# Issuing the delta-rule branch's output inside the state-space scan, with a tile tag of its own for the merge gate

## The chip, the cores and the metric

The kernel runs on one core of a Trainium2 chip, as one launch. The metric is the device time of that launch in microseconds, the median of several runs. Smaller is better.

## The reference, cut to what matters

One layer: a half-step SwiGLU feed-forward, a token mixer, a second half-step feed-forward, with 256 latent and 256 context tokens of 1024 channels. The change touches the end of the mixer only: two branches (a gated delta rule, result `o`, and a Mamba-2 state-space scan, result `y`) are gated, normalised, projected, and merged by sigmoid gates.

```python
def mixer_out(f, o, y, gdn_norm_g, mb_d, mb_norm_g, w_branch_gdn, w_branch_mb, w_out):
    za = f['zA'].reshape(b, n, GDN_HEADS, GDN_DV)
    ya = (rmsnorm(o, gdn_norm_g) * jax.nn.silu(za)).astype(dt).reshape(b, n, GDN_V)
    yb = y + mb_d.reshape(MB_GROUPS, MB_HPG)[..., None] * f['xs']
    yb = yb.reshape(...) * jax.nn.silu(f['zB'].reshape(...))
    yb = rmsnorm(yb, mb_norm_g.reshape(...)).astype(dt).reshape(b, n, MB_INNER)
    ga, gb = jnp.split(f['gates'], 2, axis=-1)
    merged = jax.nn.sigmoid(ga) * (ya @ w_branch_gdn) + jax.nn.sigmoid(gb) * (yb @ w_branch_mb)
    return merged @ w_out
```

`zA`, `zB` and `gates` are slices of the input projection `h @ w_in`.

## The kernel before, in words

**How the order comes about.** The mixer is written as a set of steps, and the string `PLAN` lists them. A number ahead of a slash sets the priority of all that follows; a smaller number goes first. The steps are issued in the order of `PLAN`, and a list scheduler then fills each engine's queue from what is ready, smaller numbers first. Two things follow from the order of issue and not from the numbers: tiles of one tag take their slots as the steps ask for them, and a step whose tile has no free slot waits for the holder. Each engine afterwards works through its own queue strictly in order, and so does SP, which starts most DMAs.

**The steps at the end of the mixer.**
- `zB5`, `g17`, `zA9` run the projections of the gates at priority 30. Each of the eight units of `zA` is eight matmuls into a PSUM tile of tag `mm` (two banks), then `zth` on ACT and DVE (L1067, L1068), then a write of `zAsc` to DRAM.
- `h40` runs the generator `ssd_all` to its end. It works on four quarters (`gi`, `hf`): `ssd_off` (state `pSs`, the sum `yg` with `xlat`, the terms `pyo` and `yo`), two `ssd_diag` (tiles `Es`, filled by a DMA from `asd`, worked on by POOL at L1429, DVE at L1431, ACT, DVE at L1442 and L1444, then the matmuls `pyd`), and `ssd_gate` (`zt`, L1456). After the second and the fourth quarter `ssd_norm` scales two quarters (`yr0`, `yr1`, L1468). The generator yields 40 times.
- `y0`, `y1` are `ssd_out`: four rounds each. A round is four transposes on PE into `pyb` (PSUM tag `tr`, one bank), then twice `ybH` on ACT (L1506) and `ybL` on DVE (L1507).
- `gdn_out` reads `zA` back from DRAM, makes `ya`, its rounded half `yaH` (ACT, L1295) and the rest `yaL` (POOL, L1296), runs the eight projections `wbg` (24 matmuls each, into `acc` of tag `mm`), and merges each with its gate `ga` into `mg` (L1302).
- `mb_out` runs the sixteen units of `wbm` against `ybH` and `ybL`, two to an accumulator, and adds `mg` (L1525, L1526).

`yg`, `xlat`, `yaH`, `yaL`, `ybH`, `ybL` and `mg` all take slots of one tag, `s4`, which has 16. `ga`, `gb`, `zA`, `zt` share tag `tL`, which has 2.

In the order lists below, a number behind a tile's name tells which tile of that name it is. `yg_8109` and `xlat_8110` are the fourth quarter's tiles before, `yg_8431` and `xlat_8432` after.

Of the kernel before, what the change touches and what calls it, by code (L numbers as in the profile page):

```python
# [6 lines left out]
F32 = mybir.dt.float32  # L7
# [7 lines left out]
P = 128  # L15
D = 1024
KD = 8
NL = 256
# [11 lines left out]
NCV = 2  # L30
POOLC = lambda t, s: False
PLAN = """10/k3 block_decay k6 5/elim 18/g5 13/dts 20/v2 g10 v7 13/m0 14/m1 13/chain_start s0 s1 m2 m3 22/q9
    B_part 27/x17 25/lat_h 22/C_part 30/zB5 g17 zA9 chain_out 13/s2 s3 14/gdn_norm 15/ssd_pre h40 51/y0 gdn_out y1 70/mb_out"""
NG = 5
GQ = 0
SSE = "gvg"
# [103 lines left out]
class Kernel:  # L140
# [1138 lines left out]
    def gdn_out(self):  # L1279

        nc, V = self.nc, self.nc.vector
        o, bc = self.o, self.bc
        yH = Ks(self, 8, NL, "yaH")
        yL = Ks(self, 8, NL, "yaL")
        for h2 in range(4):
            pv = self.smp([P, 2, NL], "pya", "ch")
            for j in range(2):
                for t in range(2):
                    nc.tensor.transpose(pv[:, j, t * P:t * P + P], o[t][:, 2 * h2 + j], self.ident)
            ya = self.t2([P, 2, NL], "ya")  # L1290
            j, hs = h2 // 2, slice(2 * (h2 % 2), 2 * (h2 % 2) + 2)
            zA = self.t2([P, 2, NL], "zA", tag="tL")
            nc.sync.dma_start(zA, self.zAsc[2 * h2:2 * h2 + 2].rearrange("m p n -> p m n"))
            V.scalar_tensor_tensor(out=ya, in0=pv, scalar=self.gng, in1=zA, op0=ALU.mult, op1=ALU.mult)
            nc.scalar.copy(yH.t[j][:, hs], ya)  # L1295
            (V if YAL[h2] == "v" else nc.gpsimd).tensor_tensor(yL.t[j][:, hs], ya, yH.t[j].bitcast(F32)[:, hs], op=ALU.subtract)  # L1296
        mg = self.mg = Ks(self, 8, NL, "mg", F32)
        for m in range(8):
            acc = self.proj("wbg", m, yH, yL, NL)
            ga = self.t2([P, NL], "ga", tag="tL")  # L1300
            nc.sync.dma_start(ga, self.gsc[m])
            V.scalar_tensor_tensor(out=mg[m], in0=ga, scalar=1.0, in1=acc, op0=ALU.add, op1=ALU.mult)  # L1302

# [329 lines left out]
```

## Time and profile before

| what | value |
| --- | --- |
| median of 3 runs | 1347.86 us (1344.52 to 1350.04) |
| the profiled execution | 1350.37 us, of it a span of 1348.6 us |
| mean granted TensorE clock in it | 0.973 |
| PE busy | 1267.5 us, 94% of the span |
| DVE busy | 977.1 us, 72% |
| ACT, POOL busy | 508.9 us (38%), 172.4 us (13%) |
| first unit of the last gate projections (`g`, then `zA`) | from 1003.87 us |
| first `wbg` matmul after the last read of `zA` | 1052.05 us |
| first merge with both `wbm` accumulators finished (L1525) | 1087.93 us |

Times inside the span count from its start. Rows of a timeline read: start, length, engine, line, operation, output, inputs, count, and in brackets the idle time just before and who ended it. The work around the change lies between about 860 and 1090 us.

### The profile page before, as it was taken

The numbers are of one execution on the slowest core, as the hardware profiler recorded it, in microseconds if no ns is written. First come the engines' busy times: TensorE is split into PE (matmuls) and PEld (weight loads), VectorE is DVE, ScalarE is ACT, GpSimd is POOL, SyncE is SP. The second block draws the span as 40 slices with busy tenths as digits, with TensorE's granted clock in tenths as the row PEclk, the third lists the DMA queues.
The fourth block names the chain that finished last, engine by engine and source line by source line (L and its number), as shares of the span: only waits on it lengthen the run. The fifth ranks groups of instructions, "written<-read, shape, count | busy, mean of one in ns | idle before, by whom it ended". The sixth has DMA issues, their size and how long they took to land.

```text
span 1348.6 us, 21052 instructions
## 1 busy us (share of the span) xinstructions
PE 1267.5 (94%) x8064; PEld 1083.8 (80%) x8064; DVE 977.1 (72%) x1692; ACT 508.9 (38%) x948; POOL 172.4 (13%) x130
## 2 busy tenths in 40 slices
PE   5889999999999997989998999998899899999997
PEld 3668888888899885779887888844468899999997
DVE  7998587646667966888778687997873466866565
ACT  3432122212236652345323565522223345544333
POOL 4200000000010231000122111333421001000000
PEclk9999999999999998999998999998999899999999
DMA  9256367636633398755542254554446556655552
GB/s 360 94 173 217 126 199 249 223 117 229 209 110 104 103 237 178 215 165 165 171 120 89 95 177 141 155 184 131 162 148 214 182 181 192 199 185 180 184 182 84
DMA packets 133016, 230.24 MB, mean 171 GB/s; under 512 B 46706, under 2 KB 78898, under 8 KB 132788
## 3 DMA queue, kind: packets, MB, share of 16 engines
q1 hardware_dynamic: 106240, 211.43, 49.7%
q10 hardware_dynamic: 26676, 17.47, 4.2%
q8 instruction: 63, 1.03, 0.3%
q14 instruction: 37, 0.30, 0.1%
HBM read 207.79 MB, written 21.07 MB: 170 GB/s over the span
## 4 chain that ended last, share of the span: by engine, by line
PE 63%; issue 17%; DVE 11%; DMA 7%; ACT 1%; POOL 1%; SPq 0%; ACTq 0%; DVEq 0%; POOLq 0%
PE acc L215 16%; PE acc L216 15%; PE acc L217 15%; PE acc L616 4%; PE acc L1054 2%; DVE junk L277 1%; DVE Es L1431 1%; DVE wlo L204 1%; PE pn L1232 1%; DMA zAsc<-zth 1%; DVE hL L440 1%; DMA Es<-asd 1%; DVE Es L1442 1%; PE pS L1258 1%; DMA raw<-in_wv 1%
## 5 line engine op out<-in xcount | busy, mean ns | idle before, releaser
L200 ACT CAST whi<-raw 128x1024 fp32r<-128x1024 f32 (+1 forms) x208 | 214.4, 1033 | 434.1 <-PE acc L216 369.4
L215 PE MATMUL acc<-hH,whi 128*128 128x512 f32 (+1 forms) x976 | 343.4, 358 | 17.2 <-ACT whi L200 8.3
L216 PE MATMUL acc<-hL,whi 128*128 128x512 f32 (+1 forms) x976 | 344.7, 355 | 4.6 <-DVE hL L440 4.6
L217 PE MATMUL acc<-hH,wlo 128*128 128x512 f32 (+1 forms) x976 | 343.3, 354 | 0.0
L204 DVE TENSOR_TENSOR wlo<-raw,whi 128x1024 fp32r<-128x1024 f32 (+1 forms) x208 | 254.4, 1225 | 93.3 <-ACT whi L200 92.0
L215 PEld LDWEIGHTS acc<-hH,whi 128*128 128x128 f32 x976 | 187.4, 192 | 43.0 <-ACT whi L200 8.6
L216 PEld LDWEIGHTS acc<-hL,whi 128*128 128x128 f32 x976 | 187.0, 192 | 30.5 <-DVE hL L440 6.9
L217 PEld LDWEIGHTS acc<-hH,wlo 128*128 128x128 f32 x976 | 186.3, 191 | 23.7
L277 DVE CUSTOM_DVE_ANT_0 junk<-wadat,cs 128x1024 f32<-128x1024 f32 x80 | 97.7, 1221 | 41.6 <-DMA wadat<-in_wadaT 40.9
L216 PE MATMUL acc<-aL,whi 128*128 128x256 f32 (+1 forms) x384 | 122.9, 323 | 0.0
L217 PE MATMUL acc<-aH,wlo 128*128 128x256 f32 (+1 forms) x384 | 122.3, 323 | 0.0
L215 PE MATMUL acc<-aH,whi 128*128 128x256 f32 (+1 forms) x384 | 122.3, 323 | 0.0
L616 PE MATMUL acc<-hF,raw 128*128 128x256 f32 x416 | 97.7, 391 | 14.6 <-ACT gth L1076 14.6
L635 DVE SCALAR_TENSOR_TENSOR cv<-cbuf,cc,cv 128x512 f32<-128x512 f32 (+1 forms) x144 | 102.0, 719 | 4.3 <-ACT cv L633 2.4
L616 PEld LDWEIGHTS acc<-hF,raw 128*128 128x128 f32 x416 | 80.3, 196 | 28.3 <-ACT gth L1076 16.0
L216 PEld LDWEIGHTS acc<-aL,whi 128*128 128x128 f32 x384 | 73.0, 190 | 5.7
L215 PEld LDWEIGHTS acc<-aH,whi 128*128 128x128 f32 x384 | 72.6, 190 | 5.7 <-DVE xc L572 0.2
L217 PEld LDWEIGHTS acc<-aH,wlo 128*128 128x128 f32 x384 | 72.7, 190 | 5.6
L382 POOL TENSOR_TENSOR sqa<-sqa,sqb 128x256 f32<-128x256 f32 x12 | 11.8, 981 | 430.5 <-ACT sqb L380 427.6
L572 DVE SCALAR_TENSOR_TENSOR xl<-acc,hg,xl 128x256 f32<-128x256 f32 x64 | 30.3, 481 | 47.3 <-PE acc L217 46.8
L1054 PE MATMUL acc<-raw,hF 128*128 128x512 f32 x128 | 59.4, 606 | 0.0
L1054 PEld LDWEIGHTS acc<-raw,hF 128*128 128x128 f32 x128 | 25.0, 197 | 30.2 <-issue 29.3
(398 smaller groups left out, 2082.3 us busy)
## 6 DMA issues: line engine op xcount, KB each, us to landing
raw<-in_wgu SPq DMA_DIRECT2D x76, 512.0 KB, 4.1
wadat<-in_wadaT SPq DMA_DIRECT2D x56, 512.0 KB, 4.1
raw<-in_wdn SPq DMA_DIRECT2D x44, 512.0 KB, 3.6
wada<-in_wada SPq DMA_DIRECT2D x16, 512.0 KB, 9.0
raw<-in_wg SPq DMA_DIRECT2D x16, 512.0 KB, 4.3
raw<-in_wxs SPq DMA_DIRECT2D x16, 512.0 KB, 3.4
Es<-asd SPq DMA_DIRECT2D x16, 512.0 KB, 4.3
raw<-in_wzB SPq DMA_DIRECT2D x16, 512.0 KB, 4.2
```

What stands on the lines that cost most here:

```text
L200: nc.scalar.copy(hi, raw)
L204: engs[i % len(engs)].tensor_tensor(lo[:, c:c + w], raw[:, c:c + w], hi[:, c:c + w].bitcast(F32), op=ALU.subtract)
L215: mm(acc, wh, xh, start=start, stop=False)
L216: mm(acc, wh, xl, start=False, stop=False)
L217: mm(acc, wl, xh, start=False, stop=stop)
L277: self.nc.vector.tensor_tensor_reduce(out=self.junk, in0=w, in1=self.cs[s], scale=1.0, scalar=0.0, op0=ALU.mult, op1=ALU.add, accum_out=out)
L440: nc.vector.scalar_tensor_tensor(out=hL[k][:, a:b], in0=u, scalar=sh[:, s:s + 1], in1=hH[k].bitcast(F32)[:, a:b], op0=ALU.add, op1=ALU.sub ...
L572: nc.vector.scalar_tensor_tensor(out=xs, in0=acc[:, NL * s - g0:NL * s - g0 + NL], scalar=hg[s][:, m:m + 1], in1=xs, op0=ALU.mult, op1=ALU ...
L616: self.nc.tensor.matmul(acc, w[:, k * P:k * P + P], self.hF[:, k], start=k == 0, stop=k == KD - 1)
L635: nc.vector.scalar_tensor_tensor(out=u3, in0=buf[:, 0:R, j:j + 64], scalar=cw[:, j:j + 1], in1=u3, op0=ALU.mult, op1=ALU.add)
L1054: nc.tensor.matmul(accs[t], self.hF[:, k, sl], w[:, wsl], start=k == 0, stop=k == 7)
L1232: nc.tensor.matmul(pn[:, j], TT[d][:, 4 * q + j], vt[q][:, j], start=True, stop=True)
```

## The change

`gdn_out` moves from behind `y0` to the middle of the scan: twelve steps of `ssd_all` are issued, then `gdn_out` at priority 40, then the other 28 steps at priority 15 as before. `ga` gets a tag of its own with two buffers.

```diff
-    B_part 27/x17 25/lat_h 22/C_part 30/zB5 g17 zA9 chain_out 13/s2 s3 14/gdn_norm 15/ssd_pre h40 51/y0 gdn_out y1 70/mb_out"""
+    B_part 27/x17 25/lat_h 22/C_part 30/zB5 g17 zA9 chain_out 13/s2 s3 14/gdn_norm 15/ssd_pre 15/h12 40/gdn_out 15/h28 51/y0 y1 70/mb_out"""
...
-            ga = self.t2([P, NL], "ga", tag="tL")
+            ga = self.tp.tile([P, NL], F32, tag="ga", bufs=2, name="ga")
```

Each engine has the same instructions as before; their order differs. PE, end of the scan: before, the fourth quarter's `pSs` stands between the third quarter's `pyd` and the last two accumulators of `zB` (`acc_7117`, `acc_7118`).

```order
 L1054 MATMUL acc_7084<-raw_7103,hF_2928 128x512
-L1375 MATMUL pSs_8093<-xw_8094,BC_6098 128x512
-L1447 MATMUL pyd_8080<-xlat_7965,Es_8049 128x64 x8
-L1375 MATMUL pSs_8093<-xw_8097,BC_6098 128x512
-L1375 MATMUL pSs_8101<-xw_8102,BC_6098 128x512
-L1447 MATMUL pyd_8168<-xlat_7965,Es_8144 128x64 x5
-L1375 MATMUL pSs_8101<-xw_8105,BC_6098 128x512
-L1447 MATMUL pyd_8168<-xlat_7965,Es_8144 128x64 x3
-L1394 MATMUL pyo_8114<-S0_8092,BC_6098 128x512
```

On the same engine now, at the end of the `wbg` projections (`acc_8327` is the last of them, `acc_8683` the first of `wbm`):

```order
+L217 MATMUL acc_8327<-yaH_8034,wlo_8324 128x256
+L1396 MATMUL pyo_8460<-Sm_8458,BC_6098 128x512
+L1397 MATMUL pyo_8460<-xo_8456,cbm_7676 128x512
+L1502 MATMUL pyb_8603<-ident_110,yg_7732 128x128 x4
+L215 MATMUL acc_8683<-ybH0_8599,whi_8686 128x256
+L215 MATMUL acc_8750<-ybH0_8599,whi_8753 128x256
+L216 MATMUL acc_8683<-ybL0_8601,whi_8686 128x256
+L217 MATMUL acc_8683<-ybH0_8599,wlo_8687 128x256
+L216 MATMUL acc_8750<-ybL0_8601,whi_8753 128x256
+L217 MATMUL acc_8750<-ybH0_8599,wlo_8754 128x256
```

The fourth quarter's off-diagonal and `pyd` matmuls and the first transposes of `y0` (`pyb_8603`), which stood ahead of and under `zA`, now end behind `wbg`, and the first `wbm` matmuls follow each round of transposes.

DVE at the same place:

```order
+L1400 TENSOR_TENSOR yg_8431<-yg_8431,yo_8463 128x512
+L1507 SCALAR_TENSOR_TENSOR ybL0_8601<-pyb_8603,cc_3243,ybH0_8599 128x256
+L1448 TENSOR_TENSOR yg_8431<-yg_8431,pyd_8539 128x512
+L1456 TENSOR_TENSOR yg_8431<-yg_8431,zt_8583 128x512
+L1507 SCALAR_TENSOR_TENSOR ybL0_8601<-pyb_8612,cc_3243,ybH0_8599 128x256
+L1462 TENSOR_TENSOR yr1_8591<-yrs_7712 128x2
+L347 TENSOR_SCALAR yr1_8591<-yr1_8591 128x2
+L1507 SCALAR_TENSOR_TENSOR ybL0_8601<-pyb_8612,cc_3243,ybH0_8599 128x256
+L1468 TENSOR_SCALAR yg_7964<-yg_7964,yr1_8591 128x512 x2
+L1468 TENSOR_SCALAR yg_8431<-yg_8431,yr1_8591 128x512 x2
+L1507 SCALAR_TENSOR_TENSOR ybL0_8602<-pyb_8621,cc_3243,ybH0_8600 128x256 x2
```

The last gate and the last norm of the scan now stand between the rounds of `y0`; before, all of them were done ahead of the first `ybL`.

SP's queue, much earlier, in the key and elimination stage near 490 us: the first two loads of `ga` now stand between DMAs that this stage needs (`Gsd` and `N` carry key products to the elimination through DRAM, `raw` is a weight tile).

```order
 L606 DMA raw_4032<-in_wg 128x1024
 L194 DMA raw_4083<-in_wv 128x1024
+L1301 DMA ga_8114<-gsc_3256 128x256
 L904 DMA Gsd_3259<-kb0_3350 128x4x128
+L1301 DMA ga_8148<-gsc_3256 128x256
 L910 DMA N_3345<-Gsd_3259 16x64x32 x2
 L194 DMA raw_4132<-in_wv 128x1024
```

They are the first users of the new tag, so nothing holds them back but the writes of `gsc` that they read; before, all eight loads of `ga` stood behind the last read of `zA`.

## The prediction

> **What bounds the kernel now.** I read the page's busy shares and chain first, then the windows over 860 to 1090 us, then the chain inside that stretch, then the timelines of PE and DVE around its gaps.
>
> ```profile
> PE 1267.5 (94%) x8064; PEld 1083.8 (80%) x8064; DVE 977.1 (72%) x1692; ACT 508.9 (38%) x948; POOL 172.4 (13%) x130
> PE 63%; issue 17%; DVE 11%; DMA 7%; ACT 1%; POOL 1%; SPq 0%; ACTq 0%; DVEq 0%; POOLq 0%
> ```
>
> PE bounds most of the span. The stages that this change touches are where it does not. Windows, columns: stretch, length, busy time of PE, PEld, DVE, ACT, POOL with counts, granted clock, DMA share, GB/s.
>
> ```profile
> 860.00:1010.00 150.00, 139.08 (x461) 80.29 (x460) 125.39 (x236) 43.55 (x101) 57.90 (x40) 0.92 0.47 154
> 1010.00:1090.00 80.00, 71.72 (x462) 66.43 (x461) 35.80 (x59) 27.90 (x44) 5.78 (x5) 0.94 0.57 184
> 930.00:940.00 10.00, 5.82 (x21) 4.30 (x20) 10.00 (x24) 2.03 (x3) 1.17 (x1) 0.72 0.28 99
> 970.00:980.00 10.00, 7.34 (x21) 4.76 (x22) 7.04 (x13) 1.17 (x2) 3.75 (x4) 0.59 0.25 92
> 1050.00:1060.00 10.00, 7.40 (x43) 7.11 (x44) 4.29 (x6) 3.36 (x4) 1.26 (x1) 0.66 0.29 96
> ```
>
> In the first stretch PE stands idle for 11 us and its clock averages 0.92, so some 12 us more go to half speed (0.08 of 150). DVE is busy 84% of it; in the second stretch only 45%. The chain of waits between 860 and 1004 us says who sets the pace (start, length, what):
>
> ```profile
> 873.32 1.72 PE pSs L1375 x4
> 884.53 0.86 PE pyo L1394 x2
> ...
> 901.89 1.28 DVE yg L1381 x2
> 910.66 5.49 DMA Es<-asd
> 916.32 1.91 POOL Es L1429
> 918.25 3.21 DVE Es L1431 x6
> 921.98 3.03 DVE Es L1431 x2
> 942.39 6.20 DMA Es<-asd
> 972.25 1.26 DVE yg L1468 x3
> 1000.52 3.52 PE pyd L1447 x32
> ```
>
> From 902 to 975 us the chain is DVE, twice broken by a load of `Es` and a POOL pass; after 975 it is PE again. The tail behind the scan hangs on the DRAM round trip of `zA`:
>
> ```profile
> 1035.70 2.54 PE L616 MATMUL acc<-hF,raw 128*128 128x256 f32 x11
> 1050.60 0.75 DVE L1294 SCALAR_TENSOR_TENSOR ya<-pya,cc,zA 128x512 f32<-128x512 f32 x1 [7.90 <-DMA zA<-zAsc]
> 1052.05 0.80 PE L215 MATMUL acc<-yaH,whi 128*128 128x256 f32 x2 [4.47 <-ACT yaH L1295]
> 1073.83 0.42 DVE L1302 SCALAR_TENSOR_TENSOR mg<-ga,acc 128x256 f32<-128x256 f32 x1 [0.65 <-PE acc L217]
> 1087.93 0.75 DVE L1525 SCALAR_TENSOR_TENSOR gb<-gb,acc 128x256 f32<-128x256 f32 x2 [0.60 <-PE acc L217]
> ```
>
> The last `zA` unit ends at 1038.2; `wbg` resumes 13.9 us later, at 1052.05; its last accumulator is read at 1073.83; both first `wbm` accumulators are read at 1087.93.
>
> **The change part by part.** What moves is not what the words say. The `wbg` matmuls need `zA`, which stays where it was, so they cannot run amid the scan. But `gdn_out` now takes its `yaH`, `yaL` and `mg` slots of tag `s4` before the last quarter takes `yg` and `xlat`. The order shows the result: the fourth quarter's `pSs`, `pyo`, `pyd`, its sum `yg`, the gates of quarters two to four, both norms and all eight `pyb` rounds go behind `zA`, most of them into and behind `wbg`.
>
> *A, the scan stretch.* Removed from DVE there (prices in columns: busy us and mean ns):
>
> ```profile
> L1400 DVE TENSOR_TENSOR yg<-yg,yo 128x512 f32<-128x512 f32 x16 | 12.7, 799 | 0.0
> L1399 DVE TENSOR_TENSOR yo<-pyo,cbm 128x512 f32<-128x512 f32 x16 | 10.7, 676 | 0.0
> L1468 DVE TENSOR_SCALAR yg<-yg,yr 128x512 f32<-128x512 f32 x4 | 1.7, 471 | 0.0
> ```
>
> Two L1381 (1.28), four `yo` and four adds (5.9), four L1456 at the price of a `yo` (2.7), four L1468 (1.7): 11.6 us, of it 5.5 before 975 us. Removed from PE: four `pSs` at 0.86 a pair of passes, six `pyo` products at 0.86, 32 `pyd` passes at 3.5, together 3.4 + 5.2 + 3.5 = 12.1 us, all after 972 us. Added: eight more `pya` transposes, 0.9. So the DVE chain gives about 5.5 us by 975 us, and PE behind it 11 more if DVE keeps ahead there, of which DVE's own 6.1 is the part that is sure. Fewer of the waits of 4 us (`Es`, 930 to 940) and less half clock are possible, since the next `Es` loads are issued sooner; I count 2 to 3 us of that. Value taken: -15. Ends: -8 (only DVE's own removals, some of them refilled by waits on `Es`) and -20 (all of PE's 12, and 8 of the 23 us of idle and lost clock).
>
> *B, under `zA`.* Four `pyb` rounds leave PE here, 16 transposes at about 0.63 for four, less the `pya` moved up:
>
> ```profile
> 1041.45 0.63 PE L1502 MATMUL pyb<-ident,yg 128*128 128x128 f32 x4 [1.78 <-DVE ybL L1507]
> ```
>
> That is 2.5 - 0.9 = 1.6, so -2 (0 to -3). The eight units stay PE-bound. `zA` should then end near 1021 instead of 1038.
>
> *C, from the last `zA` unit to the first `wbm` merges.* Before: 1087.93 - 1038.2 = 49.7 us. The round trip of 13.9 us stays; four `pSs` and two `pyo` products (5.1 us) fill its idle 4.5 us and spill 0.6. In return the half clock after the gap goes (0.66 from 1050 to 1060, and half of it before): -2. Then `wbg`: 21.8 us as before, plus 32 `pyd` passes (3.5) and four `pyo` products (3.4), plus 1 us where DVE is late: DVE's rows there now hold gates, the first norm, the fourth quarter's sums and the `wlo` that `wbg` needs. Then the rounds. Bare price of one, from these rows:
>
> ```profile
> 1085.83 0.48 DVE L1507 SCALAR_TENSOR_TENSOR ybL<-pyb,cc,ybH 128x256 fp32r<-128x256 f32 x1 [1.32 <-ACT ybH L1506]
> 1086.85 0.48 DVE L1507 SCALAR_TENSOR_TENSOR ybL<-pyb,cc,ybH 128x256 fp32r<-128x256 f32 x1 [0.54 <-ACT ybH L1506]
> ...
> L204 DVE TENSOR_TENSOR wlo<-raw,whi 128x1024 fp32r<-128x1024 f32 x14 | 17.1, 1224 | 11.1 <-ACT whi L200 11.1
> L1506 ACT ACTIVATE ybH<-pyb,cc 128x256 fp32r<-128x256 f32 x16 | 7.5, 471 | 8.8 <-PE pyb L1502 4.8 <-DVE ybL L1507 3.8
> ```
>
> Two `ybL` follow each other in 1.02 us (0.48 and 0.54 of waiting for `ybH`), and the one bank of `tr` lets no round start before the last one is read: 0.6 + 2 x 1.02 = 2.65 us, eight of them 21.2. Before, half of the rounds lay under `zA` and most of the others under `wbg`; here no other PE work stands between them but the 96 `wbm` matmuls that need them. Between the `ybL` also stand the last gate (0.7 each for L1448, L1456), the second norm (POOL, then four L1468, 1.9) and two `wlo` (2.4), of which some 4.3 us show. With 0.9 us for the last matmuls that is 26.4 us, against 1087.93 - 1073.83 = 14.1 before. C: 0.6 - 2 + 3.5 + 3.4 + 1 + 26.4 - 14.1 = +19; I take +18, since some of the early rounds' matmuls start before `wbg` is read out. Ends: +12 (bare rounds, DVE never late) and +26 (DVE late by 4 us more, the two `wlo` and the norm fully exposed at a half clock).
>
> *D, the two early `ga` loads.* They stand in SP's queue ahead of `Gsd`, `N` and a weight that is itself on the chain, and wait for their writes of `gsc`:
>
> ```profile
> 488.46 0.34 ACTq L1077 DMA_DIRECT2D gsc<-gth  x1
> ...
> DMA to landing us min/median/max: 1.7/4.4/5.9
> ...
> 493.23 5.76 DMA raw<-in_wv
> ```
>
> The second write is issued at 488.46 and lands 1.7 to 5.9 us later, so `N` and the weight go out by 0 to 1.5 us later than 493.23: +1 (0 to +2.5). The later `ga` loads stay behind `mg` as before and wait for nothing new. The own tag also frees `tL`, but `zt` now stands behind `zA` in it: each `zt` waits for a `ya` or a square, which the `wbg` stage hides.
>
> Sum: -15 - 2 + 18 + 1 = +2 us. The durations are those of the execution of 1350.37 us, which lies 2.5 us over the median of the runs; on the median of 1347.86 the sum is 1350. The bounds give -20 - 3 + 12 + 0 = -11 and -8 + 0 + 26 + 2.5 = +20.
>
> A rule that speaks against the change: the Trainium skill, "SBUF — State Buffer", section "Who interferes with whom", says that a DVE instruction with two SBUF inputs and a GpSimd instruction that reads SBUF lock each other out of a shared port for a whole instruction. The chain above agrees: two L1431 took 3.03 us from 921.98, while six, mixed, took 3.21 just before. By the rule the four POOL passes of the fourth quarter that move beside the `wlo` of `wbg` could each hold DVE up for one pass, at most the 1.91 us of the POOL row above; by it C would be up to 7.6 us dearer and the sum about +10, the time of the slower rival below. The rows of `wbg` before, with POOL nearly idle, cannot show it.
>
> **The rivals.** *Faster, by about 10 us.* DVE was the pace of the scan from 902 to 975, so with its queue shorter the `Es` loads start sooner and the idle and half clock of 930 to 940 and 970 to 980 go: A is -19, and the rounds cost near their bare price, C +12 to +13: -19 - 2 + 12 + 1 = -8, down to -11, or 1337 to 1340. For it: the clock of 0.72 and 0.59 and 4.2 us of idle in one slice. Against it: the chain's `Es` legs (5.49 + 1.91 and 6.20) are DMA and POOL, which the change does not shorten.
>
> *Slower, by about 10 us.* DVE becomes the bound between `wbg` and the first `wbm`. The work moved there (about 12 us) joins ten `wlo` (12.2), eight `mg` (3.4) and 16 `ybL` (7.7) and more: some 40 us in 54, in a fixed order, where a row that waits for `zt`, `xlat` or a POOL norm holds the next `wlo` and `mg` back, and so PE. Price: each such row 2 to 3 us, three of them +8 on C: -15 - 2 + 26 + 1 = +10, or 1358. It decides once `wbg` takes over 34 us from its resumption, where I have 30. For it: `xlat` is now loaded behind the third `wbm` weight. Against it: DVE was only 45% busy there.
>
> *The change does not do what it says.* The split of the scan could leave everything but D as it was: +1. The order speaks against that; the time would be the same verdict as mine.
>
> **How the numbers follow.** A difference of 0.5%, 6.7 us, is about what can be told from no change here. The forecast, within 0.5%: 0.43, with the no-effect case 0.05 of it. Faster rival 0.30, slower rival 0.27. Its own range for the forecast is 1343 to 1356; over all cases 1338 to 1361 leaves out a tenth at each end. Faster by over 0.5% is 0.30, within 0.43, slower 0.27.
>
> **What would show it.** In the profile after: the first `g` unit should start near 989 us instead of 1003.87 (A); the last `zA` unit should end near 1021; the gap in PE before `wbg` should be under 1 us and the clock there near 1 (C); `wbg` with its inserted `pyd` should take about 30 us; then eight rounds of `pyb` some 3 us apart with PE half idle, ending near 1090. `N` near 493 us should go out a microsecond later (D). The prediction is wrong if the first `g` unit is not earlier by at least 8 us, or if the rounds run under other PE work and cost less than 18 us.

## The result and the profile after

The changed kernel takes 1357.80 us in the median of 12 runs (1352.19 to 1362.63), the kernel before 1349.47 us in 12 runs beside them (1344.52 to 1356.79): ratio 1.0054 (1.0038 to 1.0069). That is 0.54% slower, just past the half per cent that can be told from no change. It lies in the range over all cases (1338 to 1361), but above the forecast and just above the forecast's own range (1343 to 1356): the sum said +2 us, and the two profiled executions differ by 9.15 us (1359.52 against 1350.37).

The page after, its busy shares and its chain:

```profile
PE 1269.6 (94%) x8064; PEld 1082.1 (80%) x8064; DVE 978.5 (72%) x1692; ACT 508.6 (37%) x948; POOL 174.3 (13%) x130
PE 55%; issue 17%; DVE 15%; DMA 8%; ACT 2%; POOL 1%; SPq 1%; ACTq 0%; POOLq 0%; DVEq 0%
```

The work is the same to 2 us on every engine. What grew is DVE's share of the chain (11% to 15%) and what shrank is PE's (63% to 55%): more of the time now goes where PE waits for somebody. PE's timeline after shows where (start, length, engine, line, operation, then idle time before and who ended it):

```profile
973.12 3.68 PE L1447 MATMUL pyd<-xlat,Es 128*128 128x64 f32 x16 [5.24 <-DVE Es L1444]
977.45 15.70 PE L1054 MATMUL acc<-raw,hF 128*128 128x512 f32 x32
992.99 20.88 PE L616 MATMUL acc<-hF,raw 128*128 128x256 f32 x96
...
1022.72 3.72 PE L616 MATMUL acc<-hF,raw 128*128 128x256 f32 x16 [1.06 <-DVE zth L1068]
1031.02 2.58 PE L1375 MATMUL pSs<-xw,BC 128*128 128x512 f32 x4 [3.16 <-DVE ya L1294]
1032.61 1.42 PE L215 MATMUL acc<-yaH,whi 128*128 128x256 f32 x2
...
1068.93 0.63 PE L1502 MATMUL pyb<-ident,yg 128*128 128x128 f32 x4
...
1079.07 0.63 PE L1502 MATMUL pyb<-ident,yg 128*128 128x128 f32 x4
1081.89 0.63 PE L1502 MATMUL pyb<-ident,yg 128*128 128x128 f32 x4
```

The first `g` unit starts at 992.99 instead of 1003.87, the last `zA` unit ends at 1026.4 (1022.72 + 3.72) instead of 1038.2: 11.8 us won. Then the first of the eight rounds starts at 1068.93, behind all of `wbg`, and the others follow one by one. DVE's timeline after, for the first `ybL` of one of these rounds and for the merge:

```profile
1080.24 0.48 DVE L1507 SCALAR_TENSOR_TENSOR ybL<-pyb,cc,ybH 128x256 fp32r<-128x256 f32 x1 [1.32 <-ACT ybH L1506]
...
1096.60 0.75 DVE L1525 SCALAR_TENSOR_TENSOR gb<-gb,acc 128x256 f32<-128x256 f32 x2 [0.60 <-PE acc L217]
```

Between two rounds DVE waits for ACT, ACT for the transposes on PE, and these for the bank that DVE reads last: 2.82 us from one `pyb` to the next (1079.07 to 1081.89). The first merge stands at 1096.60, 8.7 us later than the 1087.93 of before. Of the 9.15 us, 8.7 stand here; the rest of the kernel is the same to half a microsecond.

Windows after: two that answer to those of before, then `wbg` from its resumption, and the rounds (stretch, length, busy time of PE, PEld, DVE, ACT, POOL, granted clock, DMA share, GB/s):

```profile
930.00:940.00 10.00, 4.60 (x22) 2.85 (x22) 10.00 (x22) 2.03 (x3) 4.47 (x3) 1.00 0.46 159
970.00:980.00 10.00, 6.88 (x23) 5.34 (x24) 9.93 (x24) 3.22 (x9) 0.00 (x0) 0.54 0.25 82
1032.60:1068.90 36.30, 35.12 (x230) 29.34 (x229) 24.09 (x36) 12.55 (x19) 9.69 (x8) 0.96 0.58 201
1068.90:1096.60 27.70, 22.40 (x129) 17.80 (x128) 15.88 (x30) 10.84 (x23) 0.70 (x1) 0.94 0.20 67
```

In the scan the idle time and the half clock are still there (DVE full at 930 and 970, PE idle for 5.4 and 3.1 us, clock 0.54 in the second). Under `wbg` PE is 97% busy. In the rounds it is idle for 5.3 of 27.7 us by its records, which overstate its work, since a matmul that stands alone is recorded longer than one in a row (before, near 1077.6 us: 0.28 us for one `wbm` matmul, 0.40 for two in a row).

### The profile page after: what moved, and what is told of

Same layout as the page of the kernel before. It is cut to its first block, busy times and chain, and to the rows that moved or that the text cites. A ratio compares the mean times of both kernels' runs of the same rounds, so it can differ in the third digit from the quotient of the medians.

```text
span 1357.8 us, 21045 instructions
## 1 busy us (share of the span) xinstructions
PE 1269.6 (94%) x8064; PEld 1082.1 (80%) x8064; DVE 978.5 (72%) x1692; ACT 508.6 (37%) x948; POOL 174.3 (13%) x130
## 4 chain that ended last, share of the span: by engine, by line
PE 55%; issue 17%; DVE 15%; DMA 8%; ACT 2%; POOL 1%; SPq 1%; ACTq 0%; POOLq 0%; DVEq 0%
PE acc L216 14%; PE acc L215 14%; PE acc L217 14%; PE acc L616 3%; DVE cv L635 2%; DVE wlo L204 2%; DVE Es L1442 1%; DVE junk L277 1%; DVE Es L1431 1%; PE acc L1054 1%; DMA Es<-asd 1%; DMA raw<-in_wv 1%; PE pn L1232 1%; PE pS L1258 1%; DVE hL L440 1%
## 5 line engine op out<-in xcount | busy, mean ns | idle before, releaser
L382 POOL TENSOR_TENSOR sqa<-sqa,sqb 128x256 f32<-128x256 f32 x12 | 11.3, 939 | 416.5 <-ACT sqb L380 413.6
```

## The experiments

The theory: the own tag alone does nothing; the moved steps win about 11 us in the scan and lose about 20 behind it, of which most is eight rounds through one PSUM bank with nothing to cover them. Rivals: the loss is DVE's work among the `wbg` merges, or it is the displaced fourth quarter itself.

Since the kernel ahead of the scan ends a few microseconds earlier or later from one profile to the next, the table counts from the last `o` row (L1252, DVE, 859.4 before and 859.6 after) of each profile. The first column is from there to the first `g` unit, the second from there to the end of the span. The columns come from one profiled execution each, which lies up to 4 us from the median of its kernel. Ratios compare each kernel with the kernel before, run beside it; they are not the quotients of the column of medians, whose kernels before differ by up to 2.5 us.

| kernel | ratio (95% interval) | median, us | scan, us | first `g` to end, us |
| --- | --- | --- | --- | --- |
| before | 1 | 1349.47 | 144.5 | 344.7 |
| changed | 1.0054 (1.0038 to 1.0069) | 1357.80 | 133.4 | 364.8 |
| own tag alone | 1.0007 (0.9987 to 1.0027) | 1348.68 | 143.7 | 345.1 |
| moved steps alone | 1.0134 (1.0101 to 1.0168) | 1363.39 | 131.8 | 369.5 |
| changed, two banks | 1.0004 (0.9980 to 1.0028) | 1347.42 | 131.2 | 354.5 |
| before, two banks | 0.9977 (0.9954 to 1.0000) | 1345.50 | 143.5 | 341.4 |
| later split (16 steps) | 1.0133 (1.0107 to 1.0158) | 1367.43 | 148.7 | 359.6 |
| `y0` in the scan, two banks | 1.0020 (1.0005 to 1.0034) | 1351.44 | 143.3 | 345.0 |
| `y1` ahead of `gdn_out`, two banks | 0.9964 (0.9949 to 0.9980) | 1344.00 | 142.9 | 340.9 |
| the same, one bank | 0.9999 (0.9984 to 1.0014) | 1348.94 | 142.6 | 344.4 |
| changed, two banks, `zt` in tag `tA` | 0.9950 (0.9933 to 0.9967) | 1344.09 | 124.8 | 358.4 |
| `y1` ahead, two banks, `zt` in `tA` | 1.0029 (1.0009 to 1.0049) | 1353.66 | 148.9 | 343.7 |

**The two parts of the change, each alone.** Only the tag:

```diff
-            ga = self.t2([P, NL], "ga", tag="tL")
+            ga = self.tp.tile([P, NL], F32, tag="ga", bufs=2, name="ga")
```

> Only the own tag of ga; the order of the steps is that of before. My theory (the moved steps carry the whole change): within 1 us of before, at most +1.5 us through the two early ga loads in the sync queue near 490 us. Rival (the early loads or the freed tag tL carry a good part of it): +3 us or more, or a gain of 2 us or more.

Measured: ratio 1.0007, both columns as before to 0.8 us. The tag and its two early loads, which lie ahead of the scan, cost nothing that the times can tell; the interval leaves room for some 3 us either way. Only the order of the steps:

```diff
-... 15/ssd_pre h40 51/y0 gdn_out y1 70/mb_out"""
+... 15/ssd_pre 15/h12 40/gdn_out 15/h28 51/y0 y1 70/mb_out"""
```

> Only the moved steps; ga keeps its place in tag tL. My theory: as the changed kernel, +5 to +11 us over before, with the fourth quarter of the scan and all eight pyb rounds behind wbg. Rival (the own tag matters): the ga tiles now hold the two slots of tL that the gates of the scan need, so 4 us or more slower than the changed kernel; or, if the own tag is what costs, back to within 2 us of before.

Measured: 1.0134, some 0.8% above the changed kernel: the rival was right, the forecast of +5 to +11 us was too low. The loss of the change is that of the order; the tag, worth nothing before, takes part of it back once the order is there. The waits of this kernel between 1060 and 1102 us (us in total, times, longest) say by what:

```profile
PE pyb L1502 <- DVE yg L1468: 4.6, 1, 4.6
DVE yg L1456 <- DMA zt<-zsc: 4.1, 3, 1.9
```

With `ga` in `tL` its eight tiles and the gates `zt` share two slots, so the last gate is loaded late (its load goes out at 1073.54, in the changed kernel at 1049.05); DVE waits for these gates between the `ybL`, and PE stands 4.6 us for the second norm, which a transpose needs. The second column is 4.7 us longer than the changed kernel's.

**Two banks for the rounds.** The tile `pyb` alternates between tag `tr` and a second PSUM tag, `ch`, which `pya`, `pSs` and `pyo` use and which is free once these are done. "Two banks" is the name of this edit below; `ch` has two banks of its own, so up to three take turns.

```diff
-            pv = self.smp([P, 2, NL], "pyb", "tr")
+            pv = self.smp([P, 2, NL], "pyb", ("tr", "ch")[c2 % 2])
```

> The changed kernel, but the rounds of ssd_out alternate between the PSUM tags tr and ch instead of using the one bank of tr. My theory (the tail behind wbg is the serial chain of rounds through one bank): the stretch from the first pyb to the first wbm merge falls from 27.7 to 15 to 18 us, the time by 9 to 12 us below the changed kernel, so 0 to 4 us below before. Rival (the tail is the late fourth quarter on DVE and POOL, not the bank): at most 3 us off the changed kernel, still 4 us or more above before.

> The kernel before with the same two banks for the rounds. There half of the rounds lie under zA and few behind wbg. My theory: -3 to +1 us, since only the rounds after wbg (14.1 us for 11.5 us of matmuls) can shorten, and pya and pyb now share ch. Rival (one bank costs the kernel before as much as the changed one): -6 us or more.

Measured: the changed kernel goes from 1.0054 to 1.0004, about 7 us, so the whole loss is gone within the noise; this falls short of the 9 to 12 us forecast, and the rival's 3 us at most is out. The kernel before goes to 0.9977 only, about 3 us (0 to 6). PE's timeline of the changed kernel with two banks:

```profile
1061.41 1.04 PE L1502 MATMUL pyb<-ident,yg 128*128 128x128 f32 x8
...
1069.94 1.92 PE L1502 MATMUL pyb<-ident,yg 128*128 128x128 f32 x12
```

and DVE's:

```profile
1080.33 0.42 DVE L1525 SCALAR_TENSOR_TENSOR gb<-gb,acc 128x256 f32<-128x256 f32 x1 [1.70 <-PE acc L217]
```

Two rounds now follow each other at once (x8, then x12), and from the first round to the first merge it takes 18.9 us instead of 27.7, where 15 to 18 were forecast. The waits between 1060 and 1102 us, first of the changed kernel:

```profile
ACT ybH L1506 <- PE pyb L1502: 12.4, 8, 2.7
DVE ybL L1507 <- ACT ybH L1506: 10.1, 10, 1.8
```

then with two banks:

```profile
ACT ybH L1506 <- PE pyb L1502: 4.6, 4, 1.4
DVE ybL L1507 <- ACT ybH L1506: 1.0, 2, 0.8
```

So the serial hand-over through one bank is 8.8 us of this stretch in these two profiles. The Trainium skill, "Perfetto Trace Analysis", section "Matmuls", says that independent groups should go round several PSUM banks so that reading one out overlaps the next; the runs agree, with a condition beside it: the second bank is worth 0.5% where nothing else covers the rounds, and 0.2% in the kernel before, where other matmuls cover most of them.

**A later split.** After sixteen steps instead of twelve the fourth quarter takes its slots of `s4` ahead of `gdn_out`:

```diff
-... 15/h12 40/gdn_out 15/h28 51/y0 y1 70/mb_out"""
+... 15/h16 40/gdn_out 15/h24 51/y0 y1 70/mb_out"""
```

> The changed kernel with sixteen steps of the scan, not twelve, issued ahead of gdn_out: the fourth quarter's ssd_off then asks for its two slots of tag s4 before yaH, yaL and mg do. My theory (slots moved the fourth quarter, not priority 40): its pSs, pyo and pyd are back ahead of zA and none of them in wbg; the gates and six of eight rounds stay late, since zt and ybH still ask after gdn_out. First g unit at 997 to 1001 us, the time 4 to 9 us below the changed kernel, -2 to +4 us against before. Rival (issuing gdn_out inside the scan is what costs): as the changed kernel, +5 us or more over before.

Measured: 1.0133, a miss: some 18 us over before, on the rival's side, with the first `g` unit at 1006.06. The slots act as thought: the fourth quarter's `pSs`, `pyo` and half of its `pyd` stand ahead of `zA` again, and the other 16 `pyd` passes, at 1012.97, behind the first units. But PE's timeline of this kernel shows both losses at once:

```profile
940.58 10.06 PE L1054 MATMUL acc<-raw,hF 128*128 128x512 f32 x16 [8.41 <-DVE zbt L1058]
977.88 3.75 PE L1375 MATMUL pSs<-xw,BC 128*128 128x512 f32 x4 [7.75 <-ACT S L1376]
...
1056.38 0.80 PE L215 MATMUL acc<-yaH,whi 128*128 128x256 f32 x2 [4.58 <-ACT yaH L1295]
```

The scan has two waits of PE of about 8 us, the gap ahead of `wbg` is empty again (4.58 us idle), and six of the eight rounds still end behind `wbg`. So the filled gap comes from the fourth quarter's leaving, and its displacement is no pure loss. For the scan this run proves less: it is 4.2 us longer than before's, though the fourth quarter stands in both, so issuing `gdn_out` inside it costs something of its own. By what way stays open.

**`y0` early, or `y1` ahead of `gdn_out`.** If the rounds only cost where they are bare, an order that puts them under other work should be the better one. Two banks, the tag as before, and

```diff
-... 15/h12 40/gdn_out 15/h28 51/y0 y1 70/mb_out"""
+... 15/h16 51/y0 15/h24 51/gdn_out y1 70/mb_out"""
```

> Two banks for the rounds, gdn_out back behind the scan, and y0 issued after sixteen steps of it instead of after all forty. If what matters is that late work lies under zA and not behind wbg: four rounds and part of the fourth quarter move under zA, where DVE is idle over half of the time, none of the first four rounds behind wbg; 3 to 10 us below before. Rival (any work moved behind zA lengthens the end, wherever its rounds lie): 0 to +6 us.

Measured: 1.0020, a miss, since 3 to 10 us of gain were expected. PE's timeline shows why the scan did not get shorter:

```profile
942.82 9.69 PE L1054 MATMUL acc<-raw,hF 128*128 128x512 f32 x16 [8.25 <-DVE zbt L1058]
980.31 9.72 PE L1054 MATMUL acc<-raw,hF 128*128 128x512 f32 x16 [7.73 <-DVE zbt L1058]
```

PE stands for 16 us behind `zbt`, which stands late in DVE's full queue (busy without a break from 925 to 943 us). The scan is as long as in the kernel before with two banks (143.3 and 143.5 us); the other 3.6 us are in the second column (345.0 and 341.4) and are not taken apart here. Next, the whole scan and the tag as before, with `y1` ahead of `gdn_out`, so that all rounds go under `zA`; once with two banks and once with one:

```diff
-... 15/h12 40/gdn_out 15/h28 51/y0 y1 70/mb_out"""
+... 15/ssd_pre h40 51/y0 y1 gdn_out 70/mb_out"""
```

> Two banks, and y1 issued ahead of gdn_out: all eight rounds lie under zA and before wbg, none behind it. My theory: the 14.1 us from the last wbg to the first wbm merges fall to the 11.5 us of their matmuls, but pya and yaH come later behind the rounds; -1 to -5 us against before. Rival (the zA round trip then ends in a longer wait for ya, as the rounds hold ch and DVE): +2 us or more.

> The same order of steps with the one bank of tr: three rounds stand between the last zA unit and the first wbg, in the gap that is idle before. If the serial rounds cost only where nothing else covers them: within 3 us of before, and 0 to 4 us slower than with two banks. If a round costs wherever it stands: 5 us or more over before.

Measured: 0.9964 with two banks, faster than both kernels, and 0.9999 with one. Of the 0.36%, 0.23% come with the two banks alone (0.9977 in the old order), and the intervals of the two overlap, so the order by itself is not shown to gain anything. One bank instead of two costs 0.35% here. No round is left behind `wbg`; with one bank some of them stand in the gap ahead of it, and PE waits there for the bank (PE's timeline of the kernel with one bank, the longest of three waits):

```profile
1046.09 1.08 PE L1502 MATMUL pyb<-ident,yg 128*128 128x128 f32 x4 [3.73 <-DVE ybL L1507]
```

**The gates out of the shared tag.** With the order and tag of the change and two banks, `zt` moves from `tL` to the tag `tA`:

```diff
-            zt = self.t2([P, 512], "zt", tag="tL")
+            zt = self.t2([P, 512], "zt", tag="tA")
```

> The changed kernel with two banks for the rounds, and the gate tile zt in tag tA (four slots) instead of tL (two, shared with zA). The gates of quarters two and three then stand in the scan again, the fourth quarter stays late. If the gates behind zA still cost something in the tail: 2 to 6 us below the changed kernel with two banks, so 0.1 to 0.5% below before. If the tail is now PE's matmuls and the gates only load DVE in the scan: 0 to +6 us against the changed kernel with two banks.

Measured: 0.9950, the fastest of all with `y1` ahead beside it. The scan takes 124.8 us, 6.4 less than the same kernel with `zt` in `tL` and 19.7 less than before. It is not as expected, though: the gates of quarters two and three still stand behind `zA` (no L1456 between 946 and 1034 us), and the 6.4 us are no work that left, since DVE is busy for 111.5 us of this scan and for 113.1 with `zt` in `tL`. SP's queue shows where they come from. In the changed kernel the two loads of `zt` stand in it ahead of a load of `Es`, and they wait for the write of `zsc` that they read (SP's waits from 885 to 960 us: in total, times, longest):

```profile
SPq L1455 <- DMA zsc<-zbt: 7.0, 2, 6.7
```

With `zt` in `tA` the scheduler puts these loads behind four loads of `Es` (SP's timeline of this kernel, and then PE's):

```profile
906.38 0.41 SPq L1416 DMA_DIRECT2D Es<-asd  x1
...
938.87 0.86 SPq L1455 DMA_DIRECT2D zt<-zsc  x2
```

```profile
968.60 1.97 PE L1447 MATMUL pyd<-xlat,Es 128*128 128x64 f32 x16 [2.63 <-DVE Es L1444]
...
987.03 20.99 PE L616 MATMUL acc<-hF,raw 128*128 128x256 f32 x96
```

Counted from the last `o` row, this load of `Es` goes out at 44.2 us here and at 50.0 in the changed kernel (48.7 with two banks), so 4.5 of the 6.4 us are there already when it starts. PE waits 2.63 us for the last `Es`, where the changed kernel waits 5.24, and the 16 `pyd` passes behind it take 1.97 us instead of 3.68. Some of it is given back later (358.4 against 354.5 us in the second column). The same edit on the kernel with `y1` ahead:

> Two banks, y1 ahead of gdn_out, and zt in tag tA. With its gates no longer waiting for two slots, the scan's last quarter comes earlier; all rounds stay ahead of wbg. 0 to 5 us below the same kernel with zt in tL, so 0.4 to 0.7% below before. Rival (zt then takes slots from yo and ya, which hold the scan): 0 to +5 us against it.

Measured: 1.0029, 0.65% above the same kernel with `zt` in `tL`: the rival's side, and beyond its range. Of this the scan has the larger part (148.9 us against 142.9). PE's waits for `yo` from 860 to 1005 us, first with `zt` in `tL`, then in `tA`:

```profile
PE pSs L1375 <- DVE yo L1399: 6.2, 2, 3.7
PE pSs L1375 <- DVE yo L1399: 11.7, 3, 5.3
```

DVE is busy there for 130.4 us where it was for 122.6, with the same 233 rows; whether the slots that `zt` takes are behind it, as the rival has it, is not shown. DVE's timeline of this kernel, behind the scan:

```profile
1017.56 0.69 DVE L1456 TENSOR_TENSOR yg<-yg,zt 128x512 f32<-128x512 f32 x1 [6.99 <-DMA zt<-zsc]
```

DVE waits 7 us for the last gate, with the `ybL` behind it. The same line is a gain in one order and a loss in the other.

## Why the prediction came out as it did

The mechanism was right in its main parts: what leaves the scan, what comes behind `wbg`, and the rounds one by one through one bank. The sizes were off on one side, by 7 us in all, and the time came out past the half per cent to which the forecast gave 0.43, on the side that had 0.27. It lies 3 us inside the upper end of the range over all cases.

*A, the scan: -15 forecast, -10.9 measured* (1003.87 to 992.99). This is the step that failed. Of it DVE's own 11.6 us came (its rows in the scan add up to 132.6 us before and 121.0 after); of the 3.4 us counted beyond them nothing did. In busy time, where rows that overlap count once, DVE shed 9.3 us (123.8 to 114.5), and its idle time fell by 1.8 in all: the waits for `pyd` went from 5.8 us to 0.1, but "fewer of the waits of 4 us" was wrong in sign. DVE's groups by shape in the scan (busy us, mean ns, idle time before and its releaser), before:

```profile
L1431 DVE SCALAR_TENSOR_TENSOR Es<-Es,gc 128x128 f32<-128x128 f32 x48 | 20.1, 477 | 7.6 <-POOL Es L1429 7.6
```

and after:

```profile
L1431 DVE SCALAR_TENSOR_TENSOR Es<-Es,gc 128x128 f32<-128x128 f32 x48 | 20.2, 490 | 11.3 <-POOL Es L1429 11.3
```

Two waits for `Es`, 7.6 us before, are 11.3 us after. DVE has less to do and is sooner at a wait that it does not shorten. The chain after shows one of them (start, length, what):

```profile
904.85 3.86 DMA zsc<-zbt
...
908.72 0.32 SPq L1455
...
909.61 6.98 DMA Es<-asd
916.76 1.90 POOL Es L1429
918.68 5.38 DVE Es L1431 x8
```

The legs that end in this wait are a DMA and a POOL pass, as before. Ahead of them stands one that the working left out of its chain, though it is there before as well (2.34 us of `zsc<-zbt` from 907.90): the load of `Es` goes out behind the loads of `zt` (L1455), which wait for the write of the gate. A shorter queue on DVE does not shorten that leg either; `zt` in `tA` takes it away, and the scan is 6.4 us shorter. And "if DVE keeps ahead there" did not hold: the third quarter's last `pyd` waits for DVE until 973.12, and behind it in PE's queue stand 32 `zB` passes of 15.70 us and only then the first `g` unit (PE's rows after, above).

*B: -2 forecast, -0.9 measured* (11.8 in all at the end of `zA`, less A's 10.9). The transposes that left are worth 2.0 us of PE's busy time (34.3 to 32.4), and a new wait of 1.06 us for `zth`, in PE's rows after, takes half of it back. That the 2.0 agree is in part luck: four `pya` moved up and not eight, and the working subtracts them where a row that leaves should be added.

*C: +18 forecast, +20.5 measured* (1096.60 less 1026.4 is 70.2, against 49.7). To the first round it takes 42.5 us, where the stretch to the last `wbg` accumulator took 35.6: +6.9, and the terms up to there were 0.6 - 2 + 3.5 + 3.4 + 1 = +6.5. The rounds took 27.7 us where the working has 26.4. The two sizes agree to 0.4 and 1.3 us. The one thing left over is the rounding down to +18 "since some of the early rounds' matmuls start before `wbg` is read out": they do not. PE was to be half idle in the rounds; by its records it is 81% busy, but the run with two banks shows that 8.8 of the 27.7 us were the hand-over.

*D: +1 forecast.* SP's queue after, at the place of the two loads:

```profile
489.64 0.46 SPq L1301 DMA_DIRECT2D ga<-gsc  x1
...
494.00 0.74 SPq L194 DMA_DIRECT2D raw<-in_wv  x1
```

The weight goes out 0.8 us later (493.23 before); of it 0.2 us are left at the last `o` row, and A's 10.9 has them in it. The step was right, its size at the low end.

*The gap ahead of `wbg`* was to be under 1 us at a full clock. It is 3.16 us ahead of `pSs`, and the clock from 1032.6 to 1068.9 is 0.96; before, the two waits there were 7.90 us for `zA` and 4.47 for `yaH` on their engines. From the last `zA` unit to the end of `wbg` PE is idle for 4.3 us instead of 7.5, and its clock averages 0.96 instead of 0.86. The 13.9 us of the working are not one wait: before, 12 `wbg` matmuls run at once behind `zA`, as after, and some two dozen more from 1042.75 to 1047.6, and 1052.05 is where PE goes on after the wait that follows these. After, it goes on at 1032.61, 6.2 us behind `zA`, with those still to come.

*The rivals.* The faster one needed a shorter scan than DVE's own rows give; the waits for `Es` grew instead, as the argument against it had it. Its -19 for the scan was there to be had, though: with two banks and `zt` in `tA` the scan is 19.7 us shorter than before. The slower one hit the time (1358) and its condition, `wbg` over 34 us from its resumption (36.3), but not by its mechanism: in those 36.3 us DVE is busy for 24.09 and PE for 35.12. PE is the bound there, with the fourth quarter's products; `wbg` resumed 7.7 us sooner behind `zA`, with more of it left, so the same end is a longer stretch. The threshold was set for a resumption at the old distance.

*The skill's rule.* The rows show the shared port where POOL moved in. POOL's and DVE's timelines after, apart:

```profile
1062.77 1.49 POOL L1389 TENSOR_TENSOR xo<-xlat,cbm 128x512 f32<-128x512 f32 x1
1064.21 2.02 POOL L1391 TENSOR_TENSOR Sm<-S,cbm 128x512 f32<-128x512 f32 x1
```

```profile
1063.27 2.06 DVE L204 TENSOR_TENSOR wlo<-raw,whi 128x1024 fp32r<-128x1024 f32 x1
...
1068.70 1.22 DVE L204 TENSOR_TENSOR wlo<-raw,whi 128x1024 fp32r<-128x1024 f32 x1
```

A `wlo` beside POOL takes 2.06 us, one alone 1.22. It ends (1065.33) 1.07 us after the `xo` (1064.26), and the `Sm` ends (1066.23) 0.90 us after the `wlo`, as if each had waited for the one ahead to end. The Trainium skill, "SBUF — State Buffer", section "Who interferes with whom", is borne out in the duration; the 7.6 us that it would have added to C are not there, since DVE is not the bound in `wbg`. The +6.9 against +6.5 leaves 0.4 us for it at most.

That the own tag for `ga` "waits for nothing new" was right as far as it went. What the working had missed is the other side, `zt` in the old tag, of which it said that `wbg` hides its waits: with `ga` beside it the changed order is 0.8% slower, and with two banks `zt` in `tL` costs 0.5% even without `ga`.

## What to carry to other kernels

Moving steps out of a stage paid here about what the bounding engine shed (11 us) and no more: count idle time as recovered only if the change shortens the leg that ends it, and follow that leg to its start, to what stands ahead of the load in its queue. Price a chain of transposes and evictions by what covers it: eight rounds through one PSUM bank cost 8.8 us bare, and 0.2% to 0.35% (3 to 5 us) where other matmuls cover most of them; a second bank is the cheap remedy. After a change of order look again at which tiles share a tag with few slots: the same tag for `zt` was worth -0.5% in one order and +0.65% in another.

## What the runs showed of the hardware

- The granted clock falls after short waits of PE, and not at once. In the wait of 5.24 us of the changed kernel it fell about 3 us after PE had stopped (at 967.9; 0.92 from 970 to 971, 0.50 from 971), and the `pyd` behind it ran at half speed (columns as in the windows above):

```profile
973.10:976.80 3.70, 3.68 (x17) 3.68 (x18) 3.63 (x8) 0.02 (x1) 0.00 (x0) 0.50 0.03 7
```

  In the kernel with `zt` in `tA` and two banks, the same passes ran at full speed after a wait of 2.63 us, and the half speed came behind them, 4.5 us after PE had stopped and while it was busy:

```profile
968.60:970.40 1.80, 1.80 (x16) 1.80 (x16) 1.76 (x4) 0.00 (x0) 0.93 (x1) 1.00 0.07 18
970.40:974.00 3.60, 3.60 (x7) 1.60 (x7) 3.11 (x6) 0.00 (x0) 1.14 (x1) 0.53 0.77 217
```

  The Trainium skill, "TensorE: Matmul & The Clock Gate", section "What's actually happening", gives an idle window of about 3.4 us as the point where the clock halves. The first wait agrees; behind the second, shorter one the clock fell all the same, and in the kernel before a wait of 3.21 us ahead of 972.08 was enough (0.50 from 972 to 981), so a wait under that figure is not safe here.
- A DVE operation with two SBUF inputs is stretched by a busy POOL (2.06 us for 1.22), and POOL by DVE (2.02 us for the `Sm` above, 1.04 for the same operation in the kernel before at 943.60, while DVE stands idle).
- A load can be held for microseconds by another in SP's queue that waits for its data: 6.7 us for `zt` in the changed kernel, with a load of `Es` behind it.
